# One tile of the feed-forward block of a three-block transformer stack gets a second buffer

## The chip, the cores and the metric

The kernel runs on one core of a Trainium2 chip. The metric is the device time of one execution in microseconds (us), as the median of several runs. The engines are named as in the profile: PE is the matrix engine (PEld its weight loads), DVE the vector engine, ACT the scalar engine, POOL the GpSimd engine, SP the engine that issues most DMAs.

## What is computed

A sequence of 256 rows of width 1024 (float32) goes through two blocks. The first holds four feed-forward networks (FFNs) with 2816 inner columns, a gated mixer and an attention mixer; the second holds a mixer of retention and attention and a fifth FFN. What the change touches is the FFN:

```python
def swiglu(n, w_gate, w_up, w_down):
    return (jax.nn.silu(n @ w_gate) * (n @ w_up)) @ w_down

f = swiglu(rms_norm(h, ffn_pre_g[layer, 0]), ffn_w_gate[layer, 0], ffn_w_up[layer, 0], ffn_w_down[layer, 0])
h = h + 0.5 * rms_norm(f, ffn_post_g[layer, 0])
```

## The kernel before

The 256 rows are two row tiles of 128. Each is a stream of its own (`st.t` 0 and 1), and both consume the same list of weight chunks (128 x 1024), the second stream five chunks behind the first (`LAG`). In each step of the main loop one chunk is fetched by SP and cut into a high part `hi` (a cast on ACT) and a rest `lo` (a subtraction on DVE), and then each stream does its matmuls on its chunk. Each product is done as three matmuls (`mm3`, lines 168 to 170): high by high, low by high, high by low. The function `split` (lines 337 to 339) makes such pairs: line 338 is the cast, line 339 the subtraction.

An FFN has 11 units `j` of 256 inner columns. For one unit, `up` runs four chunks of matmuls into a PSUM bank `g` (two banks in all, used by both streams in turn), then a tanh on ACT (`th`, line 365) and two DVE operations (line 366, and line 368, which writes `f` and is the last to read `g`). `f` must be turned before it can be multiplied by the down weights. In most units (the first 8 of 11, in the last FFN the first 10) this goes by way of DRAM: DVE transposes blocks of 32 x 32 (`ft`, line 376), POOL issues one DMA that writes the result to the DRAM tile `far` (line 378), and four chunks later `back` allocates the tile `fr` and has POOL issue four DMAs that read it back in turned order (line 384). Two chunks after that, in program order, `parts` cuts `fr` into the pair `fth`, `ftl` by `split`; its subtraction on DVE is the last reader of `fr`. The remaining units are turned on PE (`turn`, line 399). The down-projection (`down`) of unit `j` follows two units later, two chunks each; in the first two units of an FFN, and in the last FFN at units 9 and 10, no down chunks stand between the units.

The tile framework plans the program when it is built: from priorities (program order, shifted by `urgent`) and its own estimate of when data is there, it sets the order of the instructions in each engine's queue and the waits on semaphores. A tile name with `bufs=n` has n buffers; allocating one more waits until the oldest is released by its last reader. `fr` is one name for both streams. Each engine works through its queue in that order.

Of the kernel before, what the change touches and what calls it, by code (L numbers as in the profile page):

```python
# [9 lines left out]
F32 = mybir.dt.float32  # L10
# [6 lines left out]
P = 128  # L17
# [92 lines left out]
def body(ctx: ExitStack, tc: tile.TileContext, a: dict, out: bass.AP, stop=None, dbg=None):  # L110
# [3 lines left out]
    base = ctx.enter_context(tc.tile_pool(name="base", bufs=1))  # L114
# [78 lines left out]
    def later(st, n, fn, *args):  # L193

        st.later.append([n + 1, fn, args])
# [128 lines left out]
    def acc_tile(st):  # L324
        return [psa.tile([P, 512], F32, name=f"a{st.t}{q}") for q in range(2)]

    def g_tile():
        return psg.tile([P, 512], F32, name="g")
# [8 lines left out]
    def split(hi, lo, src):  # L337
        S.copy(hi, src)  # L338
        V.tensor_tensor(lo, src, f32(hi), op=ALU.subtract)  # L339

    def rows_gemm(acc, lhs, w, k, first, last):

        for q in range(2):
            mm3(acc[q], sl(lhs, slice(None), k), sl(w, slice(None), slice(512 * q, 512 * q + 512)), first, last)

    def unit(st, ps, lhs=None, nq=4, nk=2, n=512):

        for q in range(nq):
            w = yield
            k_gemm(ps, lhs or st.xt, w, nk * q, q == 0, q == nq - 1, nk, n)  # L350
# [7 lines left out]
    def ffn(st, inner={}, last=False):  # L358
        fts = {}

        def up(j):
            ps = g_tile()
            yield from unit(st, ps)
            th = base.tile([P, 256], F32, name="th", tag="th", bufs=2)
            S.activation(th, ps[:, :256], AF.Tanh, scale=st.ch)  # L365
            V.scalar_tensor_tensor(th, th, 1.0, ps[:, :256], op0=ALU.add, op1=ALU.mult)
            f = base.tile([P, 256], F32, name="f", tag="f", bufs=2)
            V.scalar_tensor_tensor(f, th, st.cc, ps[:, 256:], op0=ALU.mult, op1=ALU.mult)  # L368
            fts[j] = f
            st.mark = f[:, 0:1]  # L370
            if j > (9 if last else 7):
                later(st, 2, turn, j)
                return

            ft = base.tile([P, 256], F32, name="ft", tag="th", bufs=2)
            V.transpose(ft, f)  # L376
            far = dram.tile([4, 32, 4, 64], F32, name="far", bufs=6)
            nc.gpsimd.dma_start(far.rearrange("a i c r -> (a i) (c r)"), ft)  # L378
            later(st, 4, back, j, far)

        def back(j, far):
            fr = base.tile([P, 4, 64], F32, name="fr", bufs=1)
            for c in range(4):
                nc.gpsimd.dma_start(fr[32 * c:32 * c + 32], far[:, :, c, :].rearrange("a i r -> i a r"))  # L384
            later(st, 1, parts, j, fr.rearrange("p a (k i) -> p k a i", k=2))

        def f_tiles(j):
            pool, n = (enter("last"), 6) if last and j > 5 else (base, 3)
            return tuple(pool.tile([P, 2, P], F32R, name=x, tag=x, bufs=n) for x in ("fth", "ftl"))

        def parts(j, fr):
            f = fts[j] = f_tiles(j)
            split(*(x.rearrange("p k (a i) -> p k a i", a=4) for x in f), fr)

        def turn(j):
            f = fts[j]
            tr = pst.tile([P, 4, P], F32, name="tr")
            for k in range(2):
                PE.transpose(tr[:, k, :], f[:, k * P:(k + 1) * P], ident)
            fts[j] = f_tiles(j)  # L400
            split(*fts[j], tr[:, :2, :])

        def down(j):
            if j == 0:
                st.acc = acc_tile(st)
            for k in range(2):
                w = yield
                f = fts[j]
                rows_gemm(st.acc, f, w, k, j + k == 0, j == NG - 1 and k == 1)

        for j in range(NG):
            yield from up(j)
            for k in downs(j, last):
                yield from down(k)
            if callable(inner.get(j)):
                inner[j]()
            elif j in inner:
                yield from inner[j]
# [614 lines left out]
    def enter(name):  # L1033
        if name not in pools:
            pools[name] = [tc.alloc_tile_pool(name=name, bufs=1), 0]
        return pools[name][0]
# [195 lines left out]
def downs(j, last):  # L1232

    if last:
        return [j - 2] if 2 <= j < 9 else [7, 8, 9, 10] if j == 10 else []
    return {0: [], 1: [], 9: [7, 8], 10: [9, 10]}.get(j, [j - 2])
# [49 lines left out]
```

## Time and profile before

| | |
|---|---|
| median of 3 runs | 1403.71 us (1401.44 to 1407.02) |
| profiled execution, own time | 1404.62 us |
| its span, first to last instruction | 1402.5 us |
| PE busy | 1363.4 us, 97% of the span |
| DVE, ACT, POOL busy | 981.2, 710.9, 293.1 us |
| write to DRAM `far`, issue to landing | 4.2 us (median of 84) |
| read-back `fr`, issue to landing | 3.7 us (median of 336) |

The profile is of one execution. A number in square brackets at the end of a timeline row is the engine's idle time before the instruction, with what ended it. Busy time of PE contains pipelined matmuls whose ends are modelled.

### The profile page before, as it was taken

The page shows a single profiled execution, that of the slowest core. Times are in us where ns is not written, and L with a number is a line of the kernel's source. Part 1 is how long each engine was busy: PE and PEld are TensorE (multiplying, and loading weights), DVE is VectorE, ACT ScalarE, POOL GpSimd, SP SyncE. Part 2 cuts the span into 40 slices and gives each one's busy share as a digit, 9 for nine tenths or more (in the row PEclk, how much of TensorE's full clock was granted, in tenths as well). Part 3 has the DMA queues.
Part 4 walks back from the last instruction along what each step waited for, and adds up shares of the span by engine and source line. Part 5 has one row for each costly group of instructions (what it writes and reads, how often), then busy time and mean ns, then how long its engine had stood idle before and what let it go on. Part 6 is the DMA issues. An engine that isn't in the chain of part 4 may idle for free. (4 is left out here: it accounts for less than half of the span.)

```text
span 1402.5 us, 18583 instructions
## 1 busy us (share of the span) xinstructions
PE 1363.4 (97%) x6234; PEld 1110.0 (79%) x6234; DVE 981.2 (70%) x1614; ACT 710.9 (51%) x1041; POOL 293.1 (21%) x501
## 2 busy tenths in 40 slices
PE   8999999999999999999999999999999999999998
PEld 5778787887788787778887887888877788778777
DVE  6776679977757658676669677766677765866554
ACT  5544456555544446444546664444567544544442
POOL 1333130000333302323201013432020000133331
PEclk9999999999999999999999999999999999999999
DMA  7777776564677764677765446777544355567763
GB/s 246 230 228 232 214 250 222 159 195 150 194 218 237 222 210 153 206 226 234 216 199 175 144 125 204 233 228 232 198 146 140 121 173 187 177 203 229 208 211 115
DMA packets 86448, 276.54 MB, mean 197 GB/s; under 512 B 15313, under 2 KB 16721, under 8 KB 85969
## 3 DMA queue, kind: packets, MB, share of 16 engines
q1 hardware_dynamic: 70992, 252.78, 57.9%
q0 software_dynamic: 14784, 22.05, 5.5%
q8 instruction: 49, 0.80, 0.2%
q10 hardware_dynamic: 576, 0.52, 0.1%
q14 instruction: 47, 0.38, 0.1%
HBM read 263.24 MB, written 12.06 MB: 196 GB/s over the span
## 5 line engine op out<-in xcount | busy, mean ns | idle before, releaser
L339 DVE TENSOR_TENSOR lo<-raw,hi 128x1024 fp32r<-128x1024 f32 (+1 forms) x462 | 560.1, 1215 | 226.5 <-ACT hi L338 225.3
L338 ACT CAST hi<-raw 128x1024 fp32r<-128x1024 f32 (+1 forms) x462 | 481.1, 1044 | 322.1 <-PE g L170 94.6
L168 PE MATMUL g<-hi,xth 128*128 128x512 f32 x1040 | 412.2, 397 | 16.5 <-DVE f L368 11.3
L169 PE MATMUL g<-lo,xth 128*128 128x512 f32 x1040 | 407.0, 392 | 2.4 <-DVE lo L339 2.4
L170 PE MATMUL g<-hi,xtl 128*128 128x512 f32 x1040 | 405.7, 392 | 1.0 <-DVE xtl L339 1.0
L384 POOL DMA_DIRECT2D fr<-far x336 | 183.4, 552 | 319.5 <-DVE ftl L339 196.7
L168 PEld LDWEIGHTS g<-hi,xth 128*128 128x128 f32 x1040 | 195.8, 188 | 66.6 <-issue 13.1
L169 PEld LDWEIGHTS g<-lo,xth 128*128 128x128 f32 x1040 | 195.8, 188 | 43.1 <-DVE lo L339 5.0
L170 PEld LDWEIGHTS g<-hi,xtl 128*128 128x128 f32 x1040 | 195.6, 188 | 42.6 <-DVE xtl L339 1.8
L168 PE MATMUL a<-hi,fth 128*128 128x512 f32 x440 | 172.3, 392 | 0.0
L170 PE MATMUL a<-hi,ftl 128*128 128x512 f32 x440 | 171.8, 390 | 0.0
L169 PE MATMUL a<-lo,fth 128*128 128x512 f32 x440 | 171.5, 390 | 0.0
L338 ACT CAST fth<-fr 128x256 fp32r<-128x256 f32 x84 | 34.2, 407 | 180.0 <-DMA fr<-far 164.4
L170 PEld LDWEIGHTS a<-hi,ftl 128*128 128x128 f32 x440 | 82.6, 188 | 17.3 <-DVE ftl L339 0.2
L169 PEld LDWEIGHTS a<-lo,fth 128*128 128x128 f32 x440 | 82.6, 188 | 16.8
L168 PEld LDWEIGHTS a<-hi,fth 128*128 128x128 f32 x440 | 82.6, 188 | 16.8
L168 PE MATMUL a<-hi,xth 128*128 128x512 f32 x232 | 93.8, 406 | 0.0
L339 DVE TENSOR_TENSOR ftl<-fr,fth 128x256 fp32r<-128x256 f32 x84 | 35.3, 420 | 80.2 <-ACT fth L338 80.1
L169 PE MATMUL a<-lo,xth 128*128 128x512 f32 x232 | 91.0, 394 | 0.0
L170 PE MATMUL a<-hi,xtl 128*128 128x512 f32 x232 | 90.9, 394 | 0.0
L378 POOL DMA_DIRECT2D far<-ft x84 | 47.6, 566 | 153.6 <-DVE ft L376 121.6
L365 ACT ACTIVATE th<-g,ch 128x256 f32<-128x256 f32 x110 | 52.0, 473 | 45.1 <-PE g L170 24.8
(322 smaller groups left out, 1290.8 us busy)
## 6 DMA issues: line engine op xcount, KB each, us to landing
raw<-in_gu SPq DMA_DIRECT2D x220, 512.0 KB, 4.3
raw<-in_dn SPq DMA_DIRECT2D x110, 512.0 KB, 4.6
raw<-in_w SPq DMA_DIRECT2D x40, 512.0 KB, 3.2
raw<-in_win SPq DMA_DIRECT2D x32, 512.0 KB, 4.0
far<-ft POOLq DMA_DIRECT2D x84, 128.0 KB, 4.2
fr<-far POOLq DMA_DIRECT2D x336, 32.0 KB, 3.7
raw<-in_wgo SPq DMA_DIRECT2D x16, 512.0 KB, 3.9
raw<-in_wo SPq DMA_DIRECT2D x8, 512.0 KB, 3.4
```

What stands on the lines that cost most here:

```text
L168: PE.matmul(o, l[0], r[0], start=start, stop=False)
L169: PE.matmul(o, l[0], r[1], start=False, stop=False)
L170: PE.matmul(o, l[1], r[0], start=False, stop=stop_)
L338: S.copy(hi, src)
L339: V.tensor_tensor(lo, src, f32(hi), op=ALU.subtract)
L365: S.activation(th, ps[:, :256], AF.Tanh, scale=st.ch)
L378: nc.gpsimd.dma_start(far.rearrange("a i c r -> (a i) (c r)"), ft)
L384: nc.gpsimd.dma_start(fr[32 * c:32 * c + 32], far[:, :, c, :].rearrange("a i r -> i a r"))
```

## The change

In `back` the tile `fr` (128 partitions x 256 float32, 1 KiB in each partition) gets two buffers instead of one. No instruction is added or taken away in the source.

```diff
@@ -379,7 +379,7 @@
             later(st, 4, back, j, far)
 
         def back(j, far):
-            fr = base.tile([P, 4, 64], F32, name="fr", bufs=1)
+            fr = base.tile([P, 4, 64], F32, name="fr", bufs=2)
             for c in range(4):
                 nc.gpsimd.dma_start(fr[32 * c:32 * c + 32], far[:, :, c, :].rearrange("a i r -> i a r"))
             later(st, 1, parts, j, fr.rearrange("p a (k i) -> p k a i", k=2))
```

## Rows read from the trace of the kernel before

**Rows 1.** The page: busy us, share of the span and instructions of each engine.
```profile
PE 1363.4 (97%) x6234; PEld 1110.0 (79%) x6234; DVE 981.2 (70%) x1614; ACT 710.9 (51%) x1041; POOL 293.1 (21%) x501
```
**Rows 2.** Busy us (instructions) by stretch: PE, PEld, DVE, ACT, POOL; clock, DMA, GB/s.
```profile
100.00:140.00 40.00, 40.00 (x178) 33.00 (x177) 24.80 (x33) 18.45 (x24) 13.72 (x25) 1.00 0.80 235
...
1320.00:1365.00 45.00, 40.61 (x176) 32.44 (x175) 28.27 (x40) 19.88 (x28) 15.30 (x29) 1.00 0.65 196
```
**Rows 3.** Waits, whole run; columns: who and for whom, us in total, times, longest.
```profile
POOL fr L384 <- DVE ftl L339: 196.7, 41, 6.7
ACT fth L338 <- DMA fr<-far: 164.4, 69, 5.0
...
PE g L168 <- DVE f L368: 11.3, 13, 2.2
```
**Rows 4.** Timeline of POOL, one pair: start us, us, line, operation [idle before <-releaser].
```profile
98.29 0.56 POOL L378 DMA_DIRECT2D far<-ft  x1 [1.92 <-DVE ft L376]
100.60 0.56 POOL L378 DMA_DIRECT2D far<-ft  x1 [1.75 <-DVE ft L376]
103.43 2.19 POOL L384 DMA_DIRECT2D fr<-far  x4 [2.28 <-DMA far<-ft]
110.53 2.17 POOL L384 DMA_DIRECT2D fr<-far  x4 [4.91 <-DVE ftl L339]
```
**Rows 5.** Timeline of ACT, the same pair and the next one's first cast.
```profile
109.38 0.41 ACT L338 CAST fth<-fr 128x256 fp32r<-128x256 f32 x1 [3.77 <-DMA fr<-far]
...
110.65 0.46 ACT L365 ACTIVATE th<-g,ch 128x256 f32<-128x256 f32 x1
...
115.99 0.41 ACT L338 CAST fth<-fr 128x256 fp32r<-128x256 f32 x1 [1.63 <-DMA fr<-far]
...
125.64 0.41 ACT L338 CAST fth<-fr 128x256 fp32r<-128x256 f32 x1 [3.03 <-DMA fr<-far]
```
**Rows 6.** The page, DMA issues: count, KB each, median us to landing.
```profile
far<-ft POOLq DMA_DIRECT2D x84, 128.0 KB, 4.2
fr<-far POOLq DMA_DIRECT2D x336, 32.0 KB, 3.7
```
**Rows 7.** Timeline of DVE around the same pair.
```profile
109.82 0.42 DVE L339 TENSOR_TENSOR ftl<-fr,fth 128x256 fp32r<-128x256 f32 x1 [2.96 <-ACT fth L338]
110.77 1.23 DVE L339 TENSOR_TENSOR lo<-raw,hi 128x1024 fp32r<-128x1024 f32 x1 [0.53 <-ACT hi L338]
...
112.36 0.48 DVE L368 SCALAR_TENSOR_TENSOR f<-th,cc,g 128x256 f32<-128x256 f32 x1
```
**Rows 8.** Timeline of PE: single matmuls that begin a group into `g`.
```profile
114.01 0.39 PE L168 MATMUL g<-hi,xth 128*128 128x512 f32 x1
...
468.77 0.47 PE L168 MATMUL g<-hi,xth 128*128 128x512 f32 x1 [0.37 <-DVE f L368]
...
588.93 0.47 PE L168 MATMUL g<-hi,xth 128*128 128x512 f32 x1 [0.90 <-ACT junk L629]
...
1327.11 0.47 PE L168 MATMUL g<-hi,xth 128*128 128x512 f32 x1 [1.60 <-DVE f L368]
...
1345.02 0.47 PE L168 MATMUL g<-hi,xth 128*128 128x512 f32 x1 [1.35 <-DVE f L368]
...
1357.13 0.47 PE L168 MATMUL g<-hi,xth 128*128 128x512 f32 x1 [0.94 <-DVE f L368]
...
1361.96 0.47 PE L168 MATMUL g<-hi,xth 128*128 128x512 f32 x1 [0.51 <-DVE f L368]
```
**Rows 9.** Timeline of POOL in the last FFN's tail.
```profile
1311.95 1.64 POOL L384 DMA_DIRECT2D fr<-far  x3 [0.19 <-issue]
1319.85 2.17 POOL L384 DMA_DIRECT2D fr<-far  x4 [6.26 <-DVE ftl L339]
```
**Rows 10.** Timeline of ACT in the last FFN's tail.
```profile
1325.21 0.41 ACT L338 CAST fth<-fr 128x256 fp32r<-128x256 f32 x1 [3.84 <-DMA fr<-far]
1325.52 0.47 ACT L365 ACTIVATE th<-g,ch 128x256 f32<-128x256 f32 x1
```

## The prediction

> **What bounds the kernel now.** I read the page's busy shares first, then busy time by stretch, then the table of waits, and last the timelines of POOL, ACT, DVE and PE around single read-backs. TensorE (PE) is busy 97% of the span [rows 1]. The stretches say where the other 3% lie: in 100 to 140 us, the middle of a feed-forward block (FFN), PE is busy 40.00 of 40 us; in 1320 to 1365 us, where the last FFN's units follow each other with no down-projection chunks between them, 40.61 of 45 us [rows 2]. So only stalls of PE are worth anything, and they sit at the edges of the FFNs.
>
> The table of waits tempts one to expect more. ACT's cast `fth` waits 164.4 us in all for the read-back to land, and POOL waits 196.7 us, 41 times, for `ftl`, the last reader of the single `fr`, before it may issue the next read-back [rows 3]. But PE's own wait that can hang on this, for `f` to be read out of the PSUM bank `g`, is 11.3 us over 13 times [rows 3]. Everything between is cover.
>
> **The pattern.** There are 84 read-backs, and in mid-FFN they come in pairs, one of each row tile; the first casts of two pairs stand 125.64 - 109.38 = 16.3 us apart [rows 5], which is one period. Take one pair. The two writes to DRAM are issued at 98.29 and 100.60. The first read-back waits only for its write (2.28 us) and is issued from 103.43 to 105.62 as four DMAs. The second waits 4.91 us for `ftl` of the first and is issued from 110.53 [rows 4]. On ACT the first cast runs at 109.38 after 3.77 us of waiting, a tanh `th` follows at 110.65, and the second cast waits 1.63 us until 115.99 [rows 5]. The buffer thus delays the second of each pair only; the first hangs on its own write.
>
> **What the edit does, step by step.** No instruction is added or removed: 84 writes, 336 read DMAs, 84 casts and 84 subtractions stay. One kind of wait goes.
>
> (1) POOL's wait. A write lands 4.2 us after issue, a read-back 3.7 us (medians) [rows 6]. The second write has landed at about 100.60 + 4.2 = 104.8; POOL is free at 105.62. So the second read-back can be issued from about 105.6 instead of 110.53, 4.9 us earlier; its fourth DMA starts near 107.2 and lands near 110.9. POOL itself gains nothing (21% busy [rows 1]), and what is queued behind there, the next `far`, waits for `ft`, not for POOL.
>
> (2) ACT's wait. With the second cast where it stands in ACT's order, 110.9 is well before it, and its 1.63 us go. In mid-FFN that pays nothing: PE is full there. The cover is the slack between `f` and PE's next use of the bank: in this period `f` ends at 112.36 + 0.48 = 112.84 and PE begins the next `g` group at 114.01 without waiting, 1.17 us later [rows 7, 8]. If that cover were gone, 1.6 us per pair would show.
>
> (3) PE's stalls. In the last FFN's tail the second cast stands ahead of a `th` that PE waits for. POOL's read-back is held 6.26 us, though POOL was free at 1311.95 + 1.64 = 1313.59, and issued at 1319.85; the cast then waits 3.84 us to 1325.21, `th` comes at 1325.52 [rows 9, 10], and PE stalls 1.60 us at 1327.11 [rows 8]. The same triple stands before the stalls of 1.35 us at 1345.02 and 0.51 at 1361.96; the one of 0.94 at 1357.13 follows a first-of-pair cast, which the edit doesn't touch [rows 8]. That makes 1.60 + 1.35 + 0.51 = 3.46 us. The stall of 0.90 us at 588.93 [rows 8] also has a buffer-held cast before it, though an ACT reading is named as its end; I count it in. Sum: 4.4 us. What is late next in the tail is the first-of-pair chain (write, read, cast), which stays.
>
> The bounds: a loss is not excluded: the planner that builds the program sets each engine's order, and a read-back that it takes to land earlier may be cast earlier (rival B). Above, all PE waits for `f`, 11.3 us [rows 3], plus the 0.90: 12.2 us. I take 4.4, since those stalls alone have the buffer wait ahead of them.
>
> The profiled execution took 1404.62 us, with 2.1 us outside its span of 1402.5. It lies 0.91 above the median of the three runs, so the sum gives 1404.62 - 4.4 = 1400.2 for such an execution and 1403.71 - 4.4 = 1399.3 for the median.
>
> In mid-FFN a gap of 4.9 us on POOL repeats once per period while PE has none [rows 2, 4]. The Trainium skill, Perfetto Trace Analysis, section Optimization Strategy, says that a gap repeating on the engine that should be saturated can mean too few buffers; the saturated engine here is PE, so by that rule the 41 waits of POOL are no reason to expect a gain, and the sum would be the tail's alone.
>
> **The rivals.** A, nothing moves: the freed read-back changes no stall, since the tail's `th` is then held by the first-of-pair cast. For it: the 0.94 us stall already has that cause. Against: the three other stalls. Time 1403.7.
>
> B, slower: a cast taken too early. ACT runs in its queue's order, and the queue puts `fth` where the read-back was expected to land. The first cast of a pair stands ahead of `th` and holds ACT 3.77 us [rows 5]. With a buffer of its own the second could be placed ahead of `th` as well. It lands near 110.9 to 111.5, so `th` moves from 110.65 to about 111.9, and DVE gets the second `ftl` (0.42 us [rows 7]) ahead of `th`. DVE is busy with a weight split until about 112.0 anyway, so `f` moves by about 0.4 us per pair. That `f` is the head of the next write and read-back: a loop of 16.3 us, as long as PE's period. So it adds up over the pairs of an FFN (84 read-backs in five FFNs make 8.4 each; the first and the last pass with less, so I take 7): 2.8 us per FFN, 14 us in five, and it costs from the pair at which the slack is used up: 1.17 us was there in the pair above, and another FFN already runs out of it (0.37 us stall at 468.77 [rows 8]). With 1.17 us absorbed in each FFN, 14 - 5.9 = 8.1 us are left, and with a third of the tail's gain kept the time is 1403.7 + 8.1 - 1.5 = 1410. The ends are 0 and the case in which the weight cast behind is pushed back too: its subtraction takes 1.23 us on DVE [rows 7], so some 1.2 + 0.4 = 1.6 us per pair, 42 x 1.6 - 5.9 = 61 us: 1465.
>
> `th` at 110.65 starts only after the waiting cast at 109.38 is done [rows 5]. The Trainium skill, PSUM — Partial Sum Buffer, section Engine vs sequencer instructions, calls the queues of ScalarE and VectorE strict FIFO; on that rests rival B, and the row agrees.
>
> C, more than the tail: ACT's and DVE's earlier return makes all 11.3 us of `f` waits go, so 1403.7 - 12.2 = 1391.5. For it: most of these stalls follow some read-back cast. Against: more than half follow first-of-pair casts or the single ones at an FFN's start, which wait for their own write.
>
> D, the edit does not do what it says: the two read-backs use one DMA queue, so the second could land late all the same. It would still be issued some 5 us earlier, and nothing in the rows holds it that long; time 1403.7, and it goes with A.
>
> **How the numbers follow.** Forecast (tail gain, 1396.5 to 1402): 0.42. A and D: 0.17. B mild (1403 to 1416): 0.22. B hard (above 1416): 0.08. C (1389 to 1396): 0.11. The likeliest time is 1399.3. A difference of 0.5% is 7 us, about what a measurement of this kernel can tell from no change (the three runs spread over 5.6 us). Faster than 1396.7: C and the forecast's edge, 0.11 + 0.06 = 0.17. Slower than 1410.7: B hard and over half of B mild, 0.08 + 0.14 = 0.22. The rest, 0.61, is within 0.5%. The range runs from 1391 (C) to 1416 (B mild); outside it lie B hard and the ends of C.
>
> **What would show it.** Right: POOL's wait for `ftl` before a read-back is near 0 instead of 196.7 us; the second read-back is issued within 0.5 us of the first one's end; the stalls near 1327, 1345 and 1362 are gone and the last stays; mid-FFN stretches still have PE full. ACT's wait for the read-back falls from 164.4 to about 98 us (41 times 1.63 us less). Rival B shows as two casts in a row ahead of a `th`, and as PE stalls `g` on `f` in mid-FFN. The forecast is wrong if the order on ACT or DVE around `fth` and `th` differs and PE is no longer full in 100 to 140 us, or if the tail's stalls stay with POOL's wait gone.

## The result and the profile after

The changed kernel takes 1412.91 us (median; 1412.42 to 1417.85) beside 1403.71 us for the kernel before in the same comparison (1401.44 to 1407.87). The ratio is 1.0067, with a 95% interval of 1.0041 to 1.0094: slower by some 9 us, where 4.4 us less had been forecast. The profiled execution took 1412.49 us, its span is 1410.4 us.

The page, busy time by engine (the line that answers to [rows 1]):

```profile
PE 1366.1 (97%) x6234; PEld 1113.0 (79%) x6234; DVE 980.0 (69%) x1614; ACT 710.3 (50%) x1041; POOL 292.8 (21%) x501
```

The same work, instruction for instruction: the counts of all five engines are those of [rows 1]. Busy time of PE grew by 2.7 us, the span by 7.9. The stretches of [rows 2], and one more between them, in which PE was busy 6.66 of 8 us in the kernel before (columns as there: stretch, us, busy us with instructions of PE, PEld, DVE, ACT, POOL, granted clock, DMA share, GB/s):

```profile
100.00:140.00 40.00, 39.57 (x174) 32.15 (x173) 23.18 (x31) 17.17 (x22) 13.70 (x25) 1.00 0.73 226
...
588.00:596.00 8.00, 5.21 (x13) 4.15 (x14) 5.30 (x10) 3.30 (x7) 1.29 (x2) 0.57 0.66 182
1320.00:1365.00 45.00, 40.31 (x177) 32.76 (x176) 25.45 (x35) 18.88 (x27) 13.15 (x25) 0.99 0.68 204
```

PE is no longer full in the middle of an FFN: 39.57 of 40 us, 174 matmuls where there were 178. The tail has no gain either. The table of waits, the lines that answer to [rows 3] (who waits for whom, us in total, times, longest):

```profile
POOL fr L384 <- DMA far<-ft: 170.8, 50, 7.6
...
ACT fth L338 <- DMA fr<-far: 137.6, 47, 6.4
...
PE g L168 <- DVE f L368: 12.8, 12, 4.5
...
PE g L168 <- DVE sm L631: 4.4, 1, 4.4
```

POOL's wait for `ftl` before a read-back (196.7 us, 41 times, in [rows 3]) has no line any more; the edit did what it says. In its place POOL waits 170.8 us for the landing of the write `far`, where that was 33.1 us before. And PE has two long waits, 4.5 and 4.4 us, where the longest for `f` had been 2.2.

What is new is the order in POOL's queue. Its timeline for the pair of [rows 4] (start us, us, line, operation, idle before and what ended it):

```profile
97.03 0.56 POOL L378 DMA_DIRECT2D far<-ft  x1 [4.58 <-DVE ft L376]
101.40 0.56 POOL L384 DMA_DIRECT2D fr<-far  x1 [3.80 <-issue]
101.94 0.56 POOL L378 DMA_DIRECT2D far<-ft  x1
102.50 1.64 POOL L384 DMA_DIRECT2D fr<-far  x3
106.78 2.18 POOL L384 DMA_DIRECT2D fr<-far  x4 [2.64 <-DMA far<-ft]
```

And DVE's transpose that makes the second write's data:

```profile
98.61 0.44 DVE L376 STREAM_TRANSPOSE ft<-f 128x256 f32<-128x256 f32 x1
```

In [rows 4] the queue runs write, write, read-back of four, read-back of four. Now it runs write, one DMA of the first read-back, the other stream's write, the other three DMAs, the second read-back. A write stands inside a read-back 34 times in the trace after, 27 of them behind its first DMA; in the one before it is 11 times and 4. The new order costs twice. The second write's data are ready at 98.61 + 0.44 = 99.05, but its turn on POOL comes behind a DMA that waits for the first write to land: it is issued at 101.94, 2.9 us late (before: 100.60, with the data ready at 100.31). And the first read-back takes 102.50 + 1.64 - 101.40 = 2.74 us to issue instead of 2.19.

Who pays for that is seen on ACT (the rows that answer to [rows 5]):

```profile
108.66 0.41 ACT L338 CAST fth<-fr 128x256 fp32r<-128x256 f32 x1 [4.21 <-DMA fr<-far]
...
109.92 0.47 ACT L365 ACTIVATE th<-g,ch 128x256 f32<-128x256 f32 x1
...
113.53 0.40 ACT L338 CAST fth<-fr 128x256 fp32r<-128x256 f32 x1
...
125.42 0.41 ACT L338 CAST fth<-fr 128x256 fp32r<-128x256 f32 x1 [3.44 <-DMA fr<-far]
```

The second cast, which had waited 1.63 us, waits for nothing now, as forecast. The first waits 4.21 us instead of 3.77, and the tanh `th` stands behind it. From the first read-back's first issue to its cast it is 108.66 - 101.40 = 7.26 us, against 109.38 - 103.43 = 5.95 before. The period between the first casts of two pairs is 16.76 us instead of 16.26. PE then waits for `f` in mid-FFN, and far longer in two places, at the edge of an FFN and near the end of the last one (the beginnings of groups into `g`, as in [rows 8]):

```profile
114.58 0.47 PE L168 MATMUL g<-hi,xth 128*128 128x512 f32 x1 [0.27 <-DVE f L368]
...
590.79 0.77 PE L168 MATMUL g<-hi,xth 128*128 128x512 f32 x1 [4.37 <-DVE sm L631]
...
1364.43 0.76 PE L168 MATMUL g<-hi,xth 128*128 128x512 f32 x1 [4.48 <-DVE f L368]
```

The stall at 1364.43 can be followed back through the pair of read-backs before it, in the tail of the last FFN. POOL first, with DVE's transpose for the second write, then ACT:

```profile
1348.12 0.56 POOL L378 DMA_DIRECT2D far<-ft  x1 [6.21 <-DVE ft L376]
1352.17 0.56 POOL L384 DMA_DIRECT2D fr<-far  x1 [3.49 <-DMA far<-ft]
1352.71 0.56 POOL L378 DMA_DIRECT2D far<-ft  x1
1353.27 1.64 POOL L384 DMA_DIRECT2D fr<-far  x3
1357.52 2.18 POOL L384 DMA_DIRECT2D fr<-far  x4 [2.61 <-DMA far<-ft]
```
```profile
1349.70 0.44 DVE L376 STREAM_TRANSPOSE ft<-f 128x256 f32<-128x256 f32 x1
```
```profile
1358.96 0.41 ACT L338 CAST fth<-fr 128x256 fp32r<-128x256 f32 x1 [2.61 <-DMA fr<-far]
...
1362.53 0.40 ACT L338 CAST fth<-fr 128x256 fp32r<-128x256 f32 x1 [2.22 <-DMA fr<-far]
1362.85 0.47 ACT L365 ACTIVATE th<-g,ch 128x256 f32<-128x256 f32 x1
...
1364.38 0.48 ACT L365 ACTIVATE th<-g,ch 128x256 f32<-128x256 f32 x1
```

The second write's data are ready at 1350.14; POOL is held until 1352.17 by the DMA that waits for the first write, and issues the second write at 1352.71. Its read-back starts at 1357.52, its cast waits until 1362.53, and the tanh that PE waits for comes behind it. The same pair in the kernel before, POOL and ACT:

```profile
1346.27 0.55 POOL L384 DMA_DIRECT2D fr<-far  x1 [3.99 <-DVE lo L339]
1346.81 0.56 POOL L378 DMA_DIRECT2D far<-ft  x1
1347.36 1.63 POOL L384 DMA_DIRECT2D fr<-far  x3
```
```profile
1353.51 0.41 ACT L338 CAST fth<-fr 128x256 fp32r<-128x256 f32 x1 [1.70 <-DMA fr<-far]
...
1354.78 0.46 ACT L365 ACTIVATE th<-g,ch 128x256 f32<-128x256 f32 x1
...
1360.06 0.41 ACT L338 CAST fth<-fr 128x256 fp32r<-128x256 f32 x1 [3.88 <-DMA fr<-far]
1360.38 0.47 ACT L365 ACTIVATE th<-g,ch 128x256 f32<-128x256 f32 x1
```

So in this pair POOL's order is not new; the write stood inside the read-back before as well. What is new is ACT's order: it ran cast, tanh, cast, tanh, and now runs cast, cast, tanh, tanh. This holds for three pairs in a row (first casts at 1324.15, 1341.26 and 1358.96). Both tanhs now stand behind the second read-back, and so a loop closes: tanh, `f`, write, read-back, cast, tanh. From the first tanh of one pair to that of the next it takes 17.77 and 18.06 us here (1327.02, 1344.79, 1362.85). In the kernel of experiment 2, where POOL's order is put back for the first of these two steps but not for the last, it takes 16.48 and then 18.64 us. The late steps add up from pair to pair, until PE has no work left that covers them.

Where the time went, by the n-th matmul of PE in both traces: the difference after minus before in its start, from one cut to the next (cuts in us of the trace before). The columns to the right are kernels of the experiments below. PE's own order is that of before but for 32 rows near 600 us in the first and third of its kernels, and 69 rows in the last. The first and third kernel have the same order in every queue up to 1250 us, and so have the second and fourth; where these differ in a stretch, by up to 2.3 us, it is the execution and not the kernel.

| stretch of before | after | write first | write first, last FFN only | write first, other FFNs only | cast behind tanh |
|---|---|---|---|---|---|
| 0 to 94 | -1.2 | -0.3 | -1.8 | -0.7 | +0.7 |
| 94 to 150, middle of FFN | +0.9 | 0.0 | +1.9 | -0.6 | -1.7 |
| 150 to 470 | -1.8 | +1.3 | +0.4 | +0.1 | 0.0 |
| 470 to 609, holds 590 | +3.1 | +0.2 | +3.0 | +2.5 | -3.8 |
| 609 to 690, middle of FFN | +2.4 | +0.4 | +2.4 | -0.1 | -0.2 |
| 690 to 850 | +0.4 | -0.6 | -0.5 | +0.9 | -0.6 |
| 850 to 974, middle of FFN | +2.4 | +1.9 | +2.8 | -0.3 | +0.5 |
| 974 to 1229 | +0.5 | +0.1 | +0.4 | 0.0 | -0.3 |
| 1229 to 1328, last FFN | -1.8 | -2.3 | -2.1 | -1.7 | -3.4 |
| 1328 to 1358, last FFN | +3.2 | -1.1 | -0.9 | +2.1 | -2.8 |
| 1358 to the end | -0.2 | -1.1 | -1.0 | +0.6 | -1.1 |
| span | +7.9 | -1.4 | +4.4 | +2.9 | -12.6 |

### The profile page after: what moved, and what is told of

Same layout as the page of the kernel before. It is cut to its first block, busy times and chain, and to the rows that moved or that the text cites. A ratio compares the mean times of both kernels' runs of the same rounds, so it can differ in the third digit from the quotient of the medians.

```text
span 1410.4 us, 18531 instructions
## 1 busy us (share of the span) xinstructions
PE 1366.1 (97%) x6234; PEld 1113.0 (79%) x6234; DVE 980.0 (69%) x1614; ACT 710.3 (50%) x1041; POOL 292.8 (21%) x501
## 5 line engine op out<-in xcount | busy, mean ns | idle before, releaser
L384 POOL DMA_DIRECT2D fr<-far x336 | 183.9, 553 | 269.1 <-DMA far<-ft 170.8
L338 ACT CAST fth<-fr 128x256 fp32r<-128x256 f32 x84 | 34.1, 406 | 159.8 <-DMA fr<-far 137.6
```

## The experiments

All ratios are to the kernel before, which ran beside each (1405.63 us beside experiments 1, 3, 4 and 5, 1404.07 beside 2 and 6, 1406.17 beside 7); between these groups, ratios compare better than medians. `tc.issue_after(x)` queues what its block issues behind x on x's engine, without waiting for the end of x.

**1. Two buffers, POOL's order in mid-FFN as before.** The read-backs of the second stream's units 1 to 6 are queued behind the other stream's write.

```diff
-            nc.gpsimd.dma_start(far.rearrange("a i c r -> (a i) (c r)"), ft)
+            shared["write"] = nc.gpsimd.dma_start(far.rearrange("a i c r -> (a i) (c r)"), ft)
...
+            with tc.issue_after(shared["write"].ins) if st.t and 1 <= j <= 6 else ExitStack():
```

> Two buffers, but POOL's order of the kernel before in mid-FFN: the second row tile's write to DRAM is issued ahead of the first row tile's read-back (units 1 to 6). Theory 1 (the planner moved that write into the middle of the first read-back, which lengthens the loop write, read, cast, tanh, f by about 0.55 us per pair): mid-FFN stalls of PE fall back to those of before, the time is about 1407 to 1408 (5 us under the changed kernel, whose other losses stay). Theory 2 (the loss is casts that stand ahead of a tanh on ACT and wait): 1411 to 1413, as the changed kernel. If neither order matters and the second buffer itself costs (DMA contention), 1411 to 1413 too, with read-backs landing as late as in the changed kernel.

Measured: 1404.25 us, ratio 0.9988 (0.9970 to 1.0006); span of the profiled execution 1401.0. POOL's timeline of the same pair, and the two stretches:

```profile
98.21 0.56 POOL L378 DMA_DIRECT2D far<-ft  x1 [7.32 <-DVE ft L376]
100.52 0.56 POOL L378 DMA_DIRECT2D far<-ft  x1 [1.75 <-DVE ft L376]
103.35 4.36 POOL L384 DMA_DIRECT2D fr<-far  x8 [2.28 <-DMA far<-ft]
```
```profile
100.00:140.00 40.00, 40.00 (x178) 33.11 (x177) 24.36 (x33) 17.57 (x23) 15.86 (x29) 1.00 0.79 241
...
1320.00:1365.00 45.00, 43.52 (x192) 35.75 (x191) 28.74 (x40) 20.57 (x27) 14.14 (x26) 1.00 0.73 209
```

On POOL this is the program that the prediction had in mind: both read-backs in one piece from 103.35, with nothing between them. The loss is gone, which is more than was expected of POOL's order (1407 to 1408 us). The stretch in mid-FFN is full, and the tail gains: PE is busy 43.52 of 45 us where it had been 40.61 [rows 2], and the last three stretches of the table give -2.3 - 1.1 - 1.1 = -4.5 us. The sum had 3.46 us for the tail; the other 0.90 of its 4.4 lay at 588.93, where PE now stalls for 3.20 us (at 590.88). The whole is not told from no change. Its +1.3 from 150 to 470 and +1.9 from 850 to 974 lie within what two executions of one order differ by. ACT's order is still the changed kernel's in the tail and at 590. So the difference of 0.79% between the two kernels comes from POOL's order, with the few rows that the planner moved along with it (13 of ACT's, 26 of DVE's, and 32 of PE's near 600 us). Both kernels have two buffers, so a slower DMA by the second buffer is not the cause.

**2. The same order in one part only.** The condition of experiment 1 with `last and` (the last FFN) or `not last and` (the four others) in front.

> The changed kernel (two buffers), with the second stream's write put back ahead of the first read-back in the last FFN alone. Theory: the changed kernel's loss has two places, the four FFNs before and the end of the last one, where a stall of 4.6 us stands at 1364 us; PE runs 4.3 us less in the last FFN of the kernel with the write first everywhere than in the changed kernel, so 1412.9 - 4.3 = 1408.6 us, between 1407 and 1410.5, and the stall at the end is under 2 us. Rival (the end of the last FFN hangs on how late the streams already are, not on the order there): 1412 to 1414, with a stall over 4 us still there.

> The changed kernel, with the second stream's write put back ahead of the first read-back in the four FFNs before the last alone. Theory: the two places add, so what the last FFN does not explain is here: 9 - 4.3 = 4.7 us, 1412.9 - 4.7 = 1408 us, between 1406 and 1410; the 4.6 us stall near the end stays, and the small stalls in the middle of the first four FFNs are gone. Rival (the middle of the FFNs is covered and the loss is at the end alone): 1412 to 1414.

Measured: last FFN alone 1410.7 us, ratio 1.0058 (1.0036 to 1.0079), span 1406.9; the others alone 1408.25 us, 1.0035 (1.0014 to 1.0057), span 1405.4. PE at the last pair, first with the last FFN's order put back, then with the others':

```profile
1362.56 0.47 PE L168 MATMUL g<-hi,xth 128*128 128x512 f32 x1 [1.69 <-DVE f L368]
```
```profile
1358.55 0.77 PE L168 MATMUL g<-hi,xth 128*128 128x512 f32 x1 [3.79 <-DVE f L368]
```

The stall at the end goes with the last FFN's order (1.69 us here, 1.49 in experiment 1, against 4.48 and 3.79 without), though the last pair itself keeps the changed kernel's order on POOL and ACT in all four. The mid-FFN losses go with the others': the three stretches "middle of FFN" sum to +5.7 and +7.1 us with the write inside the read-back, and to +2.3 and -1.0 with it put back. The spans add up: -3.5 and -5.0 us against the changed kernel, -9.3 with both. By the medians it is -2.2 and -4.7, with -8.7 for both, and by the ratios -1.3, -4.5 and -11 us; the first median lies 0.2 us outside of what was expected. The intervals are too wide to say that the parts do not add, and too wide to tell the last FFN's part from nothing in time: that it goes with POOL's order rests on the traces. The stall at 590 stays with either edit (4.94 us at 594.02 in the one, 3.53 at 590.16 in the other).

**3. The cast behind the tanh.** `parts`, which holds the cast of `fr` and its subtraction, is queued on ACT behind the last tanh that the program has issued; POOL's order is left to the planner, as in the changed kernel.

```diff
-            S.activation(th, ps[:, :256], AF.Tanh, scale=st.ch)
+            shared["th"] = S.activation(th, ps[:, :256], AF.Tanh, scale=st.ch)
...
-            split(*(x.rearrange("p k (a i) -> p k a i", a=4) for x in f), fr)
+            with tc.issue_after(shared["th"].ins): split(*(x.rearrange("p k (a i) -> p k a i", a=4) for x in f), fr)
```

> Two buffers, POOL's order free, but each cast of a read-back is queued on ACT behind the last tanh traced before it, that is in program order. Theory 2: no tanh waits behind a read-back any more; the two stalls of over 4 us (590 and 1364 us) and the mid-FFN stalls go, some 13 us of PE's waits for f, time 1395 to 1402. Theory 1: the read-back is still 0.55 us later, but it is out of the loop, so theory 1 also gives some gain in mid-FFN, about 5 us: 1407 to 1409, and the two long stalls stay.

Measured: 1392.15 us, ratio 0.9903 (0.9880 to 0.9925). ACT in the same period, the wait of the cast, and the tail:

```profile
107.79 0.47 ACT L365 ACTIVATE th<-g,ch 128x256 f32<-128x256 f32 x1
109.09 0.41 ACT L338 CAST fth<-fr 128x256 fp32r<-128x256 f32 x1 [0.82 <-DMA fr<-far]
```
```profile
ACT fth L338 <- DMA fr<-far: 26.9, 14, 3.5
```
```profile
1320.00:1365.00 45.00, 45.00 (x201) 37.19 (x200) 29.19 (x41) 21.22 (x29) 14.53 (x27) 1.00 0.75 226
```

The tanh goes first, the cast after it, and the tail is full. The gain is 3 us more than the most that was expected (1395 to 1402). POOL's wait for the write to land is 171.0 us here, as in the changed kernel, and a write still stands inside a read-back 33 times, mostly behind two of its DMAs instead of one. So nearly the same queue is harmless once no tanh stands behind the read-back. This version is faster than both kernels.

**4. Both orders together.** Experiments 1 and 3 in one kernel.

> Two buffers, both orders fixed (write first on POOL, cast behind the tanh on ACT). If the cast is out of the loop, POOL's order no longer matters and the time equals that of the kernel with the cast alone behind, within 2 us. If POOL's order costs by itself, it is 4 to 6 us faster than that one.

Measured: 1394.55 us, ratio 0.9919 (0.9901 to 0.9937). With the cast behind the tanh, putting POOL's order right gains nothing more that can be measured: it is 2.4 us slower than experiment 3, where 2 at most were expected, and the intervals overlap.

**5. One buffer, the cast behind the tanh.** The kernel before with the edit of experiment 3.

> One buffer as before, each cast queued behind the tanh. Theory 2 for the kernel before: PE's waits for f (11.3 us) go, 1392 to 1397, as fast as with two buffers. If the buffer's release then becomes the bound (the cast is later, so the next read-back is too, and its cast stands ahead of the next unit's tanh by a wait), it stays at 1400 to 1406 and the second buffer is worth 4 us or more once the casts stand right.

Measured: 1395.39 us, ratio 0.9925 (0.9907 to 0.9944). The gain is that of the cast's place. What the second buffer adds to it, 0.9925 to 0.9903, is 3 us with overlapping intervals, so it is not shown.

**6. The issue time on its own.** In the kernel before, and in that of experiment 5, the first DMA of the second stream's read-backs (units 1 to 6) is split into two halves of 16 partitions (the dose): the same bytes, five issues for four. With the cast behind the tanh the order on POOL stays as it was, and so does PE's. In the kernel before it does not quite: PE and ACT keep their order but for a few rows, yet on POOL a write stands inside a read-back 15 times instead of 11, the four new ones at the beginnings of FFNs.

```diff
-            for c in range(4):
-                nc.gpsimd.dma_start(fr[32 * c:32 * c + 32], far[:, :, c, :].rearrange("a i r -> i a r"))
+            for c, u, v in ([(0, 0, 16), (0, 16, 32)] if st.t and 1 <= j <= 6 else [(0, 0, 32)]) + [(c, 0, 32) for c in (1, 2, 3)]:
+                nc.gpsimd.dma_start(fr[32 * c + u:32 * c + v], far[:, u:v, c, :].rearrange("a i r -> i a r"))
```

> The kernel before (one buffer, cast ahead of the tanh), with one part of the read-back split: where st.t is 1 and j is 1 to 6, the first of its four DMAs is issued as two halves of 16 partitions, so five issues for the same bytes. The first read-back of a pair then keeps POOL some 0.55 us longer and lands later by that, as in the changed kernel; the write does not move. Theory (the loop f, ft, far, fr, fth, th, f is as long as PE's period, so 0.55 us in it adds up over the pairs of an FFN, less its slack): slower by 3 to 9 us, 1407 to 1413 beside a kernel before at about 1404, with PE stalls of 0.3 to 1 us for f in the middle of the FFNs and ACT's wait for the read-back up from 164 us by some 15 to 25 us. Rival (0.55 us of POOL is covered; the changed kernel's loss comes from where the casts and the second write stand): within 2 us of the kernel before, and PE full from 100 to 140 us.

> The same split of the first read-back's first DMA into two halves, in the kernel with one buffer and the cast behind the tanh (the fourth experiment, 1395.4 us). Theory: with the cast behind the tanh, f does not wait for the read-back any more, the loop is open, and 0.55 us has cover: 1394 to 1397 us, within 1.5 us of that kernel, although the same five issues stand on POOL. Rival (the extra issue costs by itself, as POOL or DMA time): as much slower than that kernel as the closed case is slower than the kernel before, 3 to 9 us, so 1398 to 1404.

Measured: in the kernel before 1412.55 us, ratio 1.0054 (1.0034 to 1.0074); with the cast behind the tanh 1399.76 us, 0.9962 (0.9946 to 0.9978). In the first, POOL's read-back and a stall of PE in mid-FFN:

```profile
102.27 2.66 POOL L384 DMA_DIRECT2D fr<-far  x5 [1.82 <-DVE lo L339]
```
```profile
115.26 0.47 PE L168 MATMUL g<-hi,xth 128*128 128x512 f32 x1 [0.40 <-DVE f L368]
```

Half a microsecond more on POOL ahead of the first read-back's end gives 8.5 us and the picture of the changed kernel, with one buffer: 39.08 us of PE in 100 to 140, ACT's wait at 193.6 us. That is the first half of the theory, though the four writes that moved on POOL may have a part in the 8.5 us. The second half failed: with the cast behind the tanh the same dose was to cost at most 1.5 us, and cost 1399.76 - 1395.39 = 4.4 (5.2 by the ratios), which lies in the rival's range. The stretch of 100 to 140 us is full there all the same. The longest stall of PE:

```profile
432.03 0.79 PE L169 MATMUL a<-lo,fth 128*128 128x512 f32 x1 [2.65 <-DVE lo L339]
```

There PE waits for a weight split, 1.57 us in experiment 5 and 2.65 here. The rest of the loss is spread over single places.

**7. The same dose with two buffers.** The dose in the kernels of experiments 1 and 4. Here POOL's order is that of these kernels, write for write, so this pair is the cleaner one; PE's order differs from theirs in 23 rows near 600 us.

> Two buffers, the write first (the first experiment, ratio 0.9988 to the kernel before), and the split of the first read-back's first DMA into two halves: 0.55 us more POOL ahead of the first read-back's end, with the cast still ahead of the tanh. Theory: the same loss as with one buffer, 5 to 10 us above the kernel with the write first, ratio 1.0025 to 1.006 to the kernel before, with stalls of PE for f near 114 and 131 us and ACT's wait for the read-back up from 128.5 us by 15 to 30. Rival (with the second buffer the dose has cover, since the second read-back is not held): ratio 0.997 to 1.001.

> Two buffers, the write first and the cast behind the tanh (the third experiment, ratio 0.9919), with the same split. The dose cost the one-buffer kernel with the cast behind the tanh some 4.4 us (1399.76 against 1395.39), against 8.5 with the loop closed, where at most 1.5 was expected. Theory: that rest hangs on the single buffer (the second read-back waits for ftl of the first, so a later first makes a later second), and with two buffers and the loop open the dose costs under 2 us: ratio 0.991 to 0.9935. Rival (an extra issue costs 4 us wherever it stands): ratio 0.9945 to 0.996.

Measured: with the cast ahead of the tanh 1407.86 us, ratio 1.0011 (0.9996 to 1.0026), against 0.9988 without the dose: some 3 us, less than the theory's 5, in between the two expectations; the interval reaches into both. With the cast behind the tanh 1396.88 us, 0.9936 (0.9915 to 0.9956), against 0.9919: 2.4 us, more than the 2 expected, and hardly to be told from zero. In the profile of the first, 100 to 140 us stays full, and another FFN's middle pays (against 25.95 of 26 us in experiment 1):

```profile
670.00:696.00 26.00, 23.83 (x104) 18.76 (x104) 17.93 (x26) 13.47 (x20) 6.52 (x12) 1.00 0.66 194
```

So the dose's price seems to hang on the second buffer at least as much as on the cast's place: 8.5 and 4.4 us with one, 3 and 2.4 with two, each within some 3 us, which is too wide to show it. With one buffer a late first read-back also makes the second late, because POOL holds it for `ftl`. For the changed kernel, which has two buffers, this puts the 0.55 us of issue time at about 3 us of its 9. The rest would then be the other price of the same order, the second write's 2.6 to 2.9 us on POOL, which the dose does not have. This split is a difference of two results and was not tested by itself; shown is that both prices together go with POOL's order (experiment 1).

## Why the prediction was wrong

**What bounds the kernel** was right: PE's stalls alone are worth anything, and POOL's 196.7 us of waiting were cover. Taking them away gained nothing by itself.

**Step (1), POOL's wait, is the step that failed.** That the wait goes was right. But the step let the second read-back start at once from 105.6, "4.9 us earlier", and said that what is queued behind on POOL, the next `far`, waits for `ft` and not for POOL. Both took the rest of POOL's order as fixed. It was not: the second read-back starts 2.6 us after the first one's end, since its own write now goes out late, and that write waits for POOL, with its data ready for 2.9 us. The "within 0.5 us" named as a sign fails in that row. Experiment 1 shows that the order makes the difference: put it back, and 0.79% of time comes back with both buffers in place. The rows to suspect it stood in the trace before, where a write already lay inside a read-back 11 times (1346.81 us above is one). Why the planner ordered it so is argued, not shown: the release of `fr` no longer holds the read-back, so it may be queued as soon as its data are estimated to be there, ahead of the other stream's write.

**Step (2), ACT's wait**, was right for the second cast of the pair shown (1.63 us to none) and wrong in sum: 137.6 us, not 98, because the first cast's wait rose, from 3.77 to 4.21 us in that pair. The "slack" of 1.17 us, which it named as the cover, is what was used up. It also left the second cast "where it stands in ACT's order", and in the tail it does not stand there any more.

**Step (3), the tail**, named the right stalls: those at 1327 and 1345 are gone in the changed kernel too (-1.8 us from 1229 to 1328). With POOL's order kept, the tail's four stalls of [rows 8], 4.40 us together, shrink to one of 1.49 at 1356.76 (experiment 1); that is 2.9 us of the 3.46 forecast there. But the step kept ACT's order as well. With the second cast ahead of both tanhs, and POOL's order in the last FFN not kept, one stall of 4.48 us takes the place of the four. The 0.90 us at 588.93, counted in, went the other way, to 4.37 us at 590.79. There, too, a cast has moved ahead of the tanh, first before, then after:

```profile
586.58 0.47 ACT L365 ACTIVATE th<-g,ch 128x256 f32<-128x256 f32 x1
...
589.42 0.41 ACT L338 CAST fth<-fr 128x256 fp32r<-128x256 f32 x1 [0.54 <-DMA fr<-far]
```
```profile
587.19 0.41 ACT L338 CAST fth<-fr 128x256 fp32r<-128x256 f32 x1 [6.42 <-DMA fr<-far]
...
588.45 0.47 ACT L365 ACTIVATE th<-g,ch 128x256 f32<-128x256 f32 x1
```

Putting POOL's order back does not mend it (3.20 us in experiment 1). The cast behind the tanh removes a good part (1.77 us at 587.31, and -3.8 us from 470 to 609).

**Rival B** had the loop (`f`, write, read-back, cast, tanh, `f`, as long as PE's period), its slack, and its sign, two casts in a row ahead of a tanh: that stands in the tail three times, and the cast at 587.19 is of the same kind. But B placed it in mid-FFN, where the second cast did not move (at 113.53 it stands behind the tanh) and a write on POOL moved instead. And with POOL's order kept, ACT's new order costs nothing on balance: experiment 1 has it in the tail and at 590, and takes the time of before. So B's price of 1410, near the 1412.9, was worked out for another place and agrees by luck. The sentence of the Trainium skill that the prediction cites for B (PSUM — Partial Sum Buffer, section Engine vs sequencer instructions) names the GpSimd engine's queue beside the two others. The rows of POOL's queue above agree: a DMA that waits for data holds an independent one behind it, and there the prediction did not look for it. A rival "POOL's order changes" was not on the list, though the profile's page had a queue of 501 instructions with two streams in it.

A reader of POOL's rows also has to keep issue and landing apart. The Trainium skill, Perfetto Trace Analysis, section DMA Instruction — SWDGE (GPSIMD), says that such a row ends when the descriptors are written, not when the data have moved. The trace agrees: the first read-back's last row ends at 104.14, its cast could start at 108.66.

The Trainium skill, Trainium Kernel Development and Optimization, section Best Practices, advises double-buffering to overlap DMA with compute. Here it cost 0.67% as it stood, nothing that can be measured with POOL's order kept (0.9988), and its worth with the cast behind the tanh (0.9925 to 0.9903) lies within the intervals.

**What stays open.** The stall at 590 us was not isolated: its read-back and its cast moved together, 32 of PE's rows behind it changed their order, and experiment 3 moved every cast. How the 9 us divide between the issue time and the late write is worked out, not tested. The 4.4 us of the dose with one buffer and the cast behind the tanh are not explained.

## What to carry to other kernels

One more buffer is a change of order, not only the end of a wait: where a planner sets the queues, ask for every queue that the freed step, or what follows from it, stands in what it may now be put ahead of (here POOL's and ACT's), and compare the order of each engine before trusting a sum made from the old one. Where an engine works in order and one of its instructions waits for a DMA, move that instruction behind the one that the bottleneck waits for: here that was worth 0.97%, with the long waits on POOL left as they were. A wait's total in the table says little; the place behind which the bottleneck's next input is queued says it.

## What was not expected of the hardware

Within the two long stalls the granted clock fell to its lower level, 1.2 GHz, and stayed there for 6.83 and 3.41 us. The windows (columns as above):

```profile
588.98:595.81 6.83, 5.02 (x12) 4.00 (x13) 4.84 (x9) 2.18 (x4) 1.29 (x2) 0.50 0.70 189
1363.81:1367.22 3.41, 2.79 (x7) 2.24 (x8) 3.37 (x6) 1.84 (x3) 0.56 (x1) 0.50 0.47 113
```

PE had been idle for 4.37 us up to 590.79 and for 4.48 us up to 1364.43. The first matmul after each stall took 0.77 and 0.76 us where the same shape at full clock takes 0.47, so such a stall costs more than its own length. A shorter stall can do it too: one of 2.17 us before and 2.14 us after has 3.41 us at the lower clock behind it in either trace (from 562.58 and 561.67 us).

The issue of a read DMA on POOL cost by the instruction here, not by its bytes: five of them, two with half the partitions, took 2.66 us, four whole ones 2.19. And where 0.47 us more of issue stood in the first read-back, the time from its first issue to its cast rose by 1.1 us (109.33 - 102.27 = 7.06 in the kernel of experiment 6 without the cast's move, 5.95 before); the rest of that was not followed further.
